# A weight row spread by transposes, a sum queued earlier and a shorter list of scans, in a hybrid decoder layer

## The chip, the cores and the metric

The kernel runs on one core of a Trainium2 chip. The metric is device time in microseconds of one execution, the median of several runs. TensorE (PE, with its weight loads as PEld), VectorE (DVE), ScalarE (ACT), GpSimd (POOL) and SyncE (SP, which issues most DMAs) each work through their own queue in order and wait for one another by semaphores.

## The reference

One decoder layer on 1024 tokens of width 1024, in float32:

```python
x = x + 0.5 * swiglu(rms_norm(x, ffn1_norm), ffn1_w_gate, ffn1_w_up, ffn1_w_down)   # d_ff 2816
h = rms_norm(x, mix_norm)
fq, fk, fv, f_logit, sq, sk, sv, g_fox, g_sb = split_columns(h @ w_in)
y_fox = forgetting_attention(rms_norm(fq), rms_norm(fk), fv, log_sigmoid(f_logit + bias))
y_sb = stick_breaking_attention(sq, sk, sv)
x = x + (sigmoid(g_fox) * (y_fox @ w_branch_fox) + sigmoid(g_sb) * (y_sb @ w_branch_sb)) @ w_out
x = x + 0.5 * swiglu(rms_norm(x, ffn2_norm), ffn2_w_gate, ffn2_w_up, ffn2_w_down)
x = x + sigmoid(rms_norm(x, ple_norm) @ w_ple_gate) * (p @ w_ple_proj)
```

Both attentions have 8 heads of 64 and are causal. In the stick-breaking one, a token's weight on an earlier one is `sigmoid(z)` times the product of `1 - sigmoid(z)` over the tokens between, which is a scan along each row of scores. `rms_norm` is `x * rsqrt(mean(x^2) + eps) * g`.

## The kernel before

Every float32 operand of a product is split into a high and a low part; a product is the sum of three (high by high, high by low, low by high). The feed-forward parts use products of sums of blocks, in an order written out by hand (`manual_schedule`): there the program's order is each engine's order.

**The entry** (`first_entry`) comes first. It loads x in eight tiles of 128 rows (`load_x`), and the weight row of the first norm into one partition of `gB`, by a DMA on ACT's queue (L1557). `busy(n)` (L253) issues n products of zeros of 128x512 in bf16, which nothing reads. `spread` (L239, L241) makes all 128 partitions of `gB` equal to the row: TensorE multiplies a column of ones with it, in two products of 512, and VectorE copies the two banks out. For each of the first four tiles `rows_stat` forms on ScalarE the mean of squares (L260, L262) and on GpSimd its power (L265), and `rows_mul` (L268, VectorE) the normed rows. `rows_high` turns a tile by eight transposes (L273) and copies the high part to `H` (L282, ScalarE); `rows_low` subtracts for the low part (L287, VectorE). `F.prep` splits weights (L600 ScalarE, L601 VectorE), and `F.plain` (L563) is the first product. In program order stand: `busy(8)`, `spread`, statistics and multiplies of four tiles, `busy(10)`, turns and splits, the first product, then the second half of x in the same way.

**Attention** is one loop over 16 heads (8 forgetting, then 8 stick-breaking), each in four steps `c` of 256 queries. Iteration `(h, c)` issues `scores` of its step, two rows of tiles of 128 queries, and between and behind them `apply` of the step two back; so the step with `c == 3` is applied while the next head's `c == 1` is scored. `fill()` puts products of other work (projections, L912 and L920) in between. Explicit order edges (`order`) hold TensorE to the program's order, and hold among themselves VectorE's scans, lower parts, sums and splits of y of the stick-breaking heads; the framework places the rest.

- `row` issues the score products (L1168, L1169), two sigmoids a bank (L1176, L1177), and leaves its scans (L1131) as parts of 256 columns in the list `pend`, sorted by step and then from the last columns to the first. A part ends with a multiply on GpSimd (L1200).
- `pop()` issues the first part of `pend`, two where more than five are pending; `pop(upto)` issues all up to a step and column.
- `apply` goes through pairs of 128 keys from the last to the first. `turn_and_scan` transposes the weights of a pair (L1228), copies the high part (L1230, ScalarE), pops scans, and subtracts for the low part (`low`, L1236, VectorE). `values` multiplies with v (L1254) into one bank, two pairs behind. At the end ScalarE copies half of the bank to y (L1280) and `add`, VectorE's sum of the other half (L1283), is left in the list `late`.
- `flush()` issues what is in `late`. After every second head, for odd `c`, `add` also calls `parts`, which splits y (L1296 ScalarE, L1297 VectorE) and issues two DMAs.

Of the kernel before, what the change touches and what calls it, by code (L numbers as in the profile page):

```python
# [10 lines left out]
F32 = mybir.dt.float32  # L11
# [7 lines left out]
P = 128  # L19
# [3 lines left out]
KD = D // P  # L23
# [13 lines left out]
def tile_hybrid_decoder_layer(  # L37
# [6 lines left out]
    nc = tc.nc  # L44
    cp = ctx.enter_context(tc.tile_pool(name="const", bufs=1))
# [10 lines left out]
    def slot(tag, shape, dt=F32):  # L56
        pad = -shape[-1] % 16
        t = sb.tile([*shape[:-1], shape[-1] + pad], dt, tag=tag, bufs=BUFS[tag], name=nm(tag))
        return t[:, :, :shape[-1]] if pad else t
# [20 lines left out]
    def pe(ins):  # L80
        order("pe", ins)
# [74 lines left out]
    nc.vector.memset(mhalf[:], -0.5)  # L156
    ones1 = cp.tile([P, 1], F32, name="ones1")
    nc.vector.memset(ones1[:], 1.0)
    gains = cp.tile([P, 3, KD], F32, name="gains")

    xd = dp.tile([KD, P, S], F32, name="x_mid")
    pd = dp.tile([KD, P, S], F32, name="p_proj")
# [67 lines left out]
    def rows_begin(X, gB):  # L230
        return {"rows": True, "x": X, "g": gB, "h": {}, "r": {}}

    def spread(gB):

        ones = slot("T", [1, P])
        nc.vector.memset(ones[:], 1.0)
        banks = [bank("sc") for _ in range(2)]
        for i, ps in enumerate(banks):
            pe(nc.tensor.matmul(ps[:], ones[:], gB[0:1, i * 512:i * 512 + 512], start=True, stop=True))  # L239
        for i, ps in enumerate(banks):  # L240
            nc.vector.tensor_copy(gB[:, i * 512:i * 512 + 512], ps[:])  # L241

# [887 lines left out]
    def scan(*args):  # L1130
        order("dve", nc.vector.tensor_tensor_scan(*args))  # L1131

    def pop(upto=None):

        n = 1 + (len(pend) > 5)
        while pend and (n if upto is None else pend[0][:2] <= upto):
            pend.pop(0)[2]()
            n -= 1
# [3 lines left out]
    def flush():  # L1142
        for call in [late.pop(0) for _ in range(len(late))]:
            call()

    def scores(step, fill):
        step["pr"] = []
        Q, KH, KL = step["st"]["st"]
        fox = step["fox"]

        def row(i):
            n = (i + 1) * P
            na, w = seg(n)
            d0 = n - P
            T = slot("T", [P, S])
            if fox:
                m = stat([P, 3], "m")
                l = stat([P, 1], "l")
                fb = step["fb"]["t"]
                nc.gpsimd.tensor_add(T[:, d0:n], fb[:, d0:n], mask_fox[:])  # L1160
                nm_ = 0
            else:
                G = slot(("GF", "RN")[i % 2], [P, S])
            for a in range(na) if fox else range(na - 1, -1, -1):
                c0, c1 = a * w, (a + 1) * w
                ps = bank("sc")
                q = Q[:, i * P:(i + 1) * P]
                pe(nc.tensor.matmul(ps[:, :w], q, KH[:, c0:c1], start=True, stop=False))  # L1168
                pe(nc.tensor.matmul(ps[:, :w], q, KL[:, c0:c1], start=False, stop=True))  # L1169
                if fox:  # L1170
                    for x0, x1, add in ((c0, min(c1, d0), fb), (max(c0, d0), c1, T)):
                        if x0 < x1:
                            nc.vector.tensor_tensor_reduce(T[:, x0:x1], add[:, x0:x1], ps[:, x0 - c0:x1 - c0], -1.0, m[:, nm_ - 1:nm_] if nm_ else 3e38, ALU.add, ALU.min, m[:, nm_:nm_ + 1])
                            nm_ += 1
                else:
                    nc.scalar.activation(G[:, c0:c1], ps[:, :w], AF.Sigmoid, scale=-(HD ** -0.5))  # L1176
                    nc.scalar.activation(T[:, c0:c1], ps[:, :w], AF.Sigmoid, scale=HD ** -0.5)  # L1177
            if fox:
                nc.scalar.activation(T[:, :n], T[:, :n], AF.Exp, bias=m[:, nm_ - 1:nm_], scale=-1.0, accum_out=l[:])
                nc.vector.reciprocal(l[:], l[:])  # L1180
                nc.gpsimd.tensor_mul(T[:, :n], T[:, :n], l[:].broadcast_to([P, n]))  # L1181
            else:
                nc.gpsimd.affine_select(T[:, d0:n], T[:, d0:n], [[-1, P]], ALU.is_ge, 0.0, base=-1, channel_multiplier=1)

                def part(kp, T=T, G=G, n=n, d0=d0):
                    c0 = kp * 256
                    c1 = min(c0 + 256, n)
                    z0 = max(c0, 1)
                    if c1 == n:
                        z1 = max(d0, 1)  # L1190
                        g = G[:, z1:n][:, ::-1]
                        scan(g, g, mask_sb[:, z1 - d0:P][:, ::-1], 1.0, ALU.mult, ALU.max)
                        if z0 < d0:
                            g = G[:, z0:d0][:, ::-1]
                            scan(g, g, g, G[:, d0:d0 + 1], ALU.mult, ALU.bypass)
                        c1 = n - 1
                    else:
                        g = G[:, z0:c1][:, ::-1]
                        scan(g, g, g, G[:, c1:c1 + 1], ALU.mult, ALU.bypass)
                    nc.gpsimd.tensor_mul(T[:, c0:c1], T[:, c0:c1], G[:, c0 + 1:c1 + 1])  # L1200
                pend.extend((step["id"], -kp, lambda kp=kp, part=part: part(kp)) for kp in range(step["c"], -1, -1))
                pend.sort(key=lambda e: e[:2])
            step["pr"].append(T)
            fill()
        for i in (2 * step["c"], 2 * step["c"] + 1):
            pop((step["id"] - 2, 0))
            pop()
            if fox or i % 2:
                flush()
            row(i)  # L1210
            yield

    def apply(step, fill):
        c = step["c"]
# [40 lines left out]

        def turn_and_scan(kpair):
            low = transposes(kpair)
            pop()
            pop((step["id"], 2 - kpair))
            low()  # L1260
            flush()
            fill()
# [285 lines left out]
    def first_entry(F):  # L1548

        X = [slot("X", [P, 4, D]) for _ in range(2)]  # L1550

        def load_x(t):
            nc.sync.dma_start(X[t // 4][:, t % 4, :], x_rows[0, t * P:(t + 1) * P, :])

        load_x(0)
        gB = slot("PT", [P, D])
        nc.scalar.dma_start(gB[0:1, :], ffn1_norm[0].unsqueeze(0))  # L1557
        nc.scalar.activation(stat([P, 1], "ss")[:], mhalf[:, 0:1], AF.Silu)
        N.append(rows_begin(X[0], gB))
        N.append(rows_begin(X[1], gB))  # L1560
        N[0]["B"] = [slot("H", [P, 2, 4, 512], F32R) for _ in range(2)]
        busy(0)
        busy(8)
        spread(N[0]["g"])
        for t in range(1, 4):
            load_x(t)
        F.load(0)
        for t in range(4, NT):
            load_x(t)
        F.load(1)  # L1570
        for i, gain in enumerate((mix_norm, ffn2_norm, ple_norm)):
            nc.sync.dma_start(gains[:, i, :], gain[0])
        for t in range(4):
            rows_stat(N[0], t, ("PT", "WL", "WL", "PT")[t], True)
            rows_mul(N[0], t)
        busy(10)
        rows_high(N[0], 0, ps1)
        rows_high(N[0], 1, ps1)
        rows_low(N[0], 0)
        F.prep(0, 1)  # L1580
        rows_high(N[0], 2, ps2)
        rows_low(N[0], 1)
        rows_high(N[0], 3, ps2)
        rows_low(N[0], 2)
        F.prep(0, 2)
        rows_stat(N[1], 0, "Y")
        rows_low(N[0], 3)
        rows_stat(N[1], 1, "Y")
        F.plain(0, 0, (0, 1), False)
        rows_mul(N[1], 0)  # L1590
        rows_stat(N[1], 2, "PT")
        rows_mul(N[1], 1)
        F.prep(0, 5)
        rows_stat(N[1], 3, "PT")
        F.prep(0, 4)
        rows_mul(N[1], 2)
        F.a(0)
        F.b(0, nc.vector)
        F.b(0)
        rows_mul(N[1], 3)  # L1600
        F.a(1)
        F.b(1, nc.vector)
        F.b(1)
        F.silu(0, 0)
        F.sums(1, nc.vector)
        F.load(2)
        for i in range(2):
            F.plain(1, 0, (i,))
            F.a(2 + i)
            F.b(2 + i, nc.vector)  # L1610
            F.b(2 + i)
            F.prep(1, 1 + i)
        F.prep(1, 5)
        ps = F.product(1, 1)
        F.t(0)
        F.evict(1, 1, ps)
        lower = F.prep(2, 1, True)
        F.t(1)
        F.l(0)
        lower()  # L1620
        ps = F.product(1, 2)
        F.t(2)
        F.l(1)
        F.t(3)
        F.l(2)
        F.evict(1, 2, ps)
        F.l(3)
        F.plain(0, 1)
        for fn in (F.u, lambda j: F.s(j, 6)):
            for j in range(2):  # L1630
                fn(j)
        F.prep(2, 2)
        F.plain(1, 1)
        for fn in (F.u, lambda j: F.s(j, 6)):
            for j in range(2, 4):
                fn(j)
        F.prep(1, 6)
# [218 lines left out]
```

## Time and profile before

| | us |
|---|---|
| median of 3 runs | 2238.27 (2237.66 to 2238.58) |
| the profiled execution | 2238.81 |
| its span | 2237.1 |
| busy TensorE / weight loads | 2214.9 / 1880.1 |
| busy VectorE | 1517.7 |
| busy ScalarE | 1006.2 |
| busy GpSimd | 822.8 |

In rows of the timeline the first number is the start in us from the span's start, the second the time from the first start to the last end, then engine, line, operation, tiles (out <- in), shapes and count; in brackets the idle time before it and what ended it. Rows of the stretches give, for each engine in turn (PE, PEld, DVE, ACT, POOL), busy time and instructions, then the granted clock, the DMA engines' share and GB/s. Rows of the waits give total us, times and the longest.

### The profile page before, as it was taken

The numbers are of one execution on the slowest core, as the hardware profiler recorded it, in microseconds if no ns is written. First come the engines' busy times: TensorE is split into PE (matmuls) and PEld (weight loads), VectorE is DVE, ScalarE is ACT, GpSimd is POOL, SyncE is SP. The second block draws the span as 40 slices with busy tenths as digits, with TensorE's granted clock in tenths as the row PEclk, the third lists the DMA queues.
The fourth block names the chain that finished last, engine by engine and source line by source line (L and its number), as shares of the span: only waits on it lengthen the run. The fifth ranks groups of instructions, "written<-read, shape, count | busy, mean of one in ns | idle before, by whom it ended". The sixth has DMA issues, their size and how long they took to land.

```text
span 2237.1 us, 30542 instructions
## 1 busy us (share of the span) xinstructions
PE 2214.9 (99%) x11212; PEld 1880.1 (84%) x11212; DVE 1517.7 (68%) x2367; ACT 1006.2 (45%) x1805; POOL 822.8 (37%) x788
## 2 busy tenths in 40 slices
PE   9999999999999999999999999999999999999999
PEld 7888888888888899999898888888888888888887
DVE  8855545598888324666677885789655555688888
ACT  6433333433455435555566663255333333333454
POOL 1344534210021336566567664520544444200021
PEclk9999999999999999999999999999999999999999
DMA  3332323394322334333323465741423232574336
GB/s 133 104 127 81 132 80 132 114 347 171 117 95 100 128 107 130 86 104 86 85 53 95 119 203 185 262 174 57 141 81 125 77 120 93 199 262 174 113 113 169
DMA packets 195607, 294.89 MB, mean 132 GB/s; under 512 B 28665, under 2 KB 108793, under 8 KB 195458
## 3 DMA queue, kind: packets, MB, share of 16 engines
q1 hardware_dynamic: 194448, 289.80, 39.3%
q0 software_dynamic: 1008, 3.15, 0.8%
q8 instruction: 88, 1.44, 0.3%
q14 instruction: 61, 0.50, 0.1%
q10 hardware_dynamic: 2, 0.00, 0.0%
HBM read 192.99 MB, written 83.13 MB: 123 GB/s over the span
## 4 chain that ended last, share of the span: by engine, by line
PE 93%; DVE 3%; ACT 2%; POOL 1%; issue 1%; DMA 0%; SPq 0%; ACTq 0%; DVEq 0%; POOLq 0%
PE ps L627 43%; PE ps L509 22%; PE ps L912 8%; PE ps L920 5%; PE ps L563 4%; PE ps L1523 3%; PE ps L1254 2%; PE ps L1228 2%; PE ps L1169 1%; PE ps L1168 1%; PE ps L1074 1%; DVE PT L1236 1%; DVE RN L1131 1%; DVE GF L1131 1%; POOL WL L139 0%
## 5 line engine op out<-in xcount | busy, mean ns | idle before, releaser
L509 PE MATMUL ps<-H,H 128*128 128x512 f32 x2184 | 497.3, 389 | 0.0
L509 PEld LDWEIGHTS ps<-H,H 128*128 128x128 f32 x2184 | 409.5, 188 | 84.8
L627 PE MATMUL ps<-H,WL 128*128 128x512 f32 x1164 | 275.0, 389 | 0.0
L627 PEld LDWEIGHTS ps<-H,WL 128*128 128x128 f32 x1164 | 218.5, 188 | 45.3
L185 POOL TENSOR_TENSOR PT<-PT,PT 128x512 f32<-128x512 f32 x27 | 34.9, 1294 | 403.9 <-ACT PT L182 403.0
L627 PE MATMUL ps<-H,Q 128*128 128x512 f32 x624 | 148.4, 389 | 0.0
L517 DVE SCALAR_TENSOR_TENSOR X<-ps,X 128x512 f32<-128x512 f32 x168 | 110.2, 685 | 47.2 <-PE ps L509 47.1
L627 PE MATMUL ps<-X,WL 128*128 128x512 f32 x576 | 138.3, 389 | 0.0
L627 PEld LDWEIGHTS ps<-H,Q 128*128 128x128 f32 x624 | 117.1, 188 | 24.3
L1236 DVE TENSOR_TENSOR PT<-ps,PT 128x512 fp32r<-128x512 f32 (+1 forms) x160 | 99.9, 628 | 44.2 <-ACT PT L1230 43.5
L627 PE MATMUL ps<-H,PT 128*128 128x512 f32 x540 | 128.9, 389 | 0.0
L627 PEld LDWEIGHTS ps<-X,WL 128*128 128x128 f32 x576 | 108.1, 188 | 22.4
L139 POOL TENSOR_TENSOR WL<-RAW,WH 128x512 fp32r<-128x512 f32 (+1 forms) x84 | 97.6, 1181 | 74.0 <-ACT WH L129 46.5
L412 POOL TENSOR_TENSOR PT<-GF,RN 128x512 f32<-128x512 f32 x20 | 33.5, 1674 | 236.8 <-DVE GF L820 236.8
L627 PEld LDWEIGHTS ps<-H,PT 128*128 128x128 f32 x540 | 101.2, 188 | 21.1
L912 PE MATMUL ps<-WH,H 128*128 128x256 f32 x768 | 116.1, 288 | 0.8 <-ACT RN L977 0.8
L920 PE MATMUL ps<-H,WH 128*128 128x512 f32 x384 | 115.0, 406 | 0.0
L1254 PE MATMUL ps<-PT,X 128*128 128x256 f32 (+1 forms) x640 | 102.4, 286 | 9.5 <-DVE PT L1236 8.6
L1230 ACT CAST PT<-ps 128x512 fp32r<-128x512 f32 (+1 forms) x160 | 87.2, 548 | 44.6 <-PE ps L1228 40.5
L1254 PEld LDWEIGHTS ps<-PT,X 128*128 128x128 f32 x640 | 90.3, 190 | 19.9 <-DVE PT L1236 13.4
L912 PEld LDWEIGHTS ps<-WH,H 128*128 128x128 f32 x768 | 101.5, 190 | 2.6 <-ACT RN L977 1.2
L1181 POOL TENSOR_TENSOR T<-T,l 128x128 f32<-128x128 f32 (+3 forms) x64 | 73.2, 1147 | 67.5 <-DVE l L1180 65.4
(453 smaller groups left out, 4795.9 us busy)
## 6 DMA issues: line engine op xcount, KB each, us to landing
hidden<-PT SPq DMA_DIRECT2D x40, 512.0 KB, 3.1
WH<-in_ffn_w_gate_dram SPq DMA_DIRECT2D x38, 512.0 KB, 5.5
Q<-hidden SPq DMA_DIRECT2D x24, 512.0 KB, 5.6
hidden<-RN SPq DMA_DIRECT2D x22, 512.0 KB, 2.6
KH<-in_ffn_w_up_dram SPq DMA_DIRECT2D x20, 512.0 KB, 6.2
KL<-in_ffn_w_up_dram SPq DMA_DIRECT2D x20, 512.0 KB, 6.9
T<-in_ffn_w_down_dram SPq DMA_DIRECT2D x20, 512.0 KB, 7.1
GF<-hidden SPq DMA_DIRECT2D x14, 512.0 KB, 7.0
```

What stands on the lines that cost most here:

```text
L139: ins = eng_lo.tensor_sub(lo[part], raw[part], f(hi[part]))
L509: pe(nc.tensor.matmul(groups[g][t][:], wt[:, b, k, t * P:(t + 1) * P], act[:, a, k, :], start=(fresh and n == 0), stop=(i in (6, 1, 4) and ...
L517: nc.vector.scalar_tensor_tensor(xs, groups[g][t][:], scale, xs, ALU.mult, ALU.add)
L563: pe(nc.tensor.matmul(ps[:], hl[:, a, k, :], right(rb, b, k), start=(i == 0), stop=(i == 23)))
L627: pe(nc.tensor.matmul(ps[:, cols], hl[:, a, k, :], right(B[m], b, k)[:, cols], start=(first and i == 0), stop=(final and i == 11), skip_gr ...
L912: pe(nc.tensor.matmul(ps[:, :n], hT[t // 4](a, k)[:, (t % 4) * P:(t % 4 + 1) * P], w[k // 4][b][:, k % 4, :n], start=(i == 0), stop=(i == ...
L920: pe(nc.tensor.matmul(ps[:], w[a][:, k, :], hT[half](b, k), start=(i == 0), stop=(i == 23)))
L1181: nc.gpsimd.tensor_mul(T[:, :n], T[:, :n], l[:].broadcast_to([P, n]))
L1230: high = nc.scalar.copy(pt[:, 0, :width], ps[:, :width])
L1236: ins = nc.vector.tensor_sub(pt[:, 1, :width], ps[:, :width], f(pt[:, 0, :width]))
L1254: pe(nc.tensor.matmul(o, lh, r, start=(kpair == c and i == 0), stop=(kpair == 0 and i == 3)))
L1523: pe(nc.tensor.matmul(ps[:], w[a][:, k, :], yT[g][b][:, k, half * 512:half * 512 + 512], start=(i == 0), stop=(i == 11)))
```

## The change

1. The weight of the first norm is laid out on the host as eight columns of 128 and loaded into `gains[:, 3, :]`, still from ACT's queue. `spread` makes the full rows by eight transposes of a column broadcast along the free axis, four to a bank. `busy(8)` before it becomes `busy(9)`, `busy(10)` behind the multiplies `busy(6)`. The memset of ones goes.
2. In `scores`, `flush()` is called ahead of both rows of a stick-breaking step; it was called ahead of the second alone. The sum of y left by the step before, and its split where there is one, then stand ahead of the first row.
3. `turn_and_scan` pops one part, not one or two, at the last two turns of a step with `c == 3`.

```diff
-    gains = cp.tile([P, 3, KD], F32, name="gains")
+    gains = cp.tile([P, 4, KD], F32, name="gains")
...
-    def spread(gB):
-
-        ones = slot("T", [1, P])
-        nc.vector.memset(ones[:], 1.0)
+    def spread(gB, col):
+
         banks = [bank("sc") for _ in range(2)]
-        for i, ps in enumerate(banks):
-            pe(nc.tensor.matmul(ps[:], ones[:], gB[0:1, i * 512:i * 512 + 512], start=True, stop=True))
+        for k in range(KD):
+            pe(nc.tensor.transpose(banks[k // 4][:, k % 4 * P:(k % 4 + 1) * P], col[:, k:k + 1].broadcast_to([P, P]), identf[:]))
         for i, ps in enumerate(banks):
             nc.vector.tensor_copy(gB[:, i * 512:i * 512 + 512], ps[:])
...
-    def pop(upto=None):
-
-        n = 1 + (len(pend) > 5)
+    def pop(upto=None, n=None):
+
+        n = n or 1 + (len(pend) > 5)
...
-            if fox or i % 2:
-                flush()
+            flush()
             row(i)
...
-            pop()
+            pop(n=1 if c == 3 and kpair < 2 else None)
             pop((step["id"], 2 - kpair))
...
-        nc.scalar.dma_start(gB[0:1, :], ffn1_norm[0].unsqueeze(0))
+        nc.scalar.dma_start(gains[:, 3, :], ffn1_norm[0])
...
-        busy(8)
-        spread(N[0]["g"])
+        busy(9)
+        spread(N[0]["g"], gains[:, 3, :])
...
-        busy(10)
+        busy(6)
...
-        elif name in ("mix_norm", "ffn2_norm", "ple_norm"):
+        elif name in ("ffn1_norm", "mix_norm", "ffn2_norm", "ple_norm"):
```

## The prediction

> **What bounds the kernel now.** I read the page first, then stretches, then the first 25 us engine by engine, then the waits and single steps of the stick-breaking part.
>
> ```profile
> span 2237.1 us, 30542 instructions
> ...
> PE 2214.9 (99%) x11212; PEld 1880.1 (84%) x11212; DVE 1517.7 (68%) x2367; ACT 1006.2 (45%) x1805; POOL 822.8 (37%) x788
> ...
> PE 93%; DVE 3%; ACT 2%; POOL 1%; issue 1%; DMA 0%; SPq 0%; ACTq 0%; DVEq 0%; POOLq 0%
> ```
> ```profile
> 50.00:635.00 585.00, 585.00 (x2585) 484.14 (x2584) 386.50 (x453) 218.36 (x337) 177.02 (x122) 1.00 0.39 136
> ...
> 1100.00:1345.00 245.00, 236.95 (x1448) 207.98 (x1447) 192.89 (x328) 154.20 (x339) 159.96 (x234) 1.00 0.42 115
> ```
>
> TensorE is the bound: 93% of the chain, and full from 50 to 635 us, where nothing of the diff runs. So an edit gains only where TensorE idles or does work that it need not: the first 18 us, and the stick-breaking part (1100 to 1345 us), where it is idle for 245 - 236.95 = 8 us. What is saved before 50 us is carried through the full stretch unchanged.
>
> **The entry (first edit).** The rows of TensorE:
>
> ```profile
> 1.32 3.59 PE L253 MATMUL ps<-T 128*128 128x512 bf16 x8 [1.32 <-DVE T L249]
> 4.84 3.78 PE L239 MATMUL ps<-PT,T 1*128 1x512 f32 x4
> 8.55 4.45 PE L253 MATMUL ps<-T 128*128 128x512 bf16 x10
> 12.79 1.67 PE L273 MATMUL ps<-identf,PT 128*128 128x128 f32 x8
> 14.30 1.91 PE L273 MATMUL ps<-identf,WL 128*128 128x128 f32 x16
> ...
> 18.09 5.78 PE L563 MATMUL ps<-H,WL 128*128 128x512 f32 x24 [1.01 <-ACT H L282]
> 23.71 1.91 PE L273 MATMUL ps<-identf,Y 128*128 128x128 f32 x16
> ```
>
> Filler products (L253) step by (12.79 - 8.55)/10 = 0.424 us; the same width at L563 steps by (23.71 - 18.09)/24 = 0.234. The first transposes take 0.21 each, the next sixteen 1.91/16 = 0.12. So the array runs at half pace until some point among the first transposes, though the column PEclk of the stretches reads 1.00: here the pace tells, not that column. What opens it matters below.
>
> ScalarE, then VectorE, GpSimd and the DMAs:
>
> ```profile
> 4.47 1.06 ACT L260 ACTIVATE PT<-X 128x1024 f32<-128x1024 f32 x1 [1.62 <-DMA X<-in_x_rows_dram]
> ...
> 7.72 1.06 ACT L260 ACTIVATE WL<-X 128x1024 f32<-128x1024 f32 x1 [0.55 <-DMA X<-in_x_rows_dram]
> ...
> 10.20 0.20 ACT L262 ACTIVATE ss<-ss 128x1 f32<-128x1 f32 x1
> 13.89 2.17 ACT L282 CAST H<-ps 128x512 fp32r<-128x512 f32 x4 [3.49 <-PE ps L273]
> 15.94 0.64 ACT L600 CAST WL<-WH 128x512 fp32r<-128x512 f32 x1
> 16.45 2.08 ACT L282 CAST H<-ps 128x512 fp32r<-128x512 f32 x4
> 18.36 0.68 ACT L600 CAST WL<-WH 128x512 fp32r<-128x512 f32 x1
> ```
> ```profile
> 8.66 0.69 DVE L241 COPY PT<-ps 128x512 f32<-128x512 f32 x1 [1.01 <-PE ps L239]
> 9.45 1.28 DVE L268 SCALAR_TENSOR_TENSOR PT<-X,rt,PT 128x1024 f32<-128x1024 f32 x1
> ...
> 13.04 1.28 DVE L268 SCALAR_TENSOR_TENSOR PT<-X,rt,PT 128x1024 f32<-128x1024 f32 x1
> ...
> 17.22 2.48 DVE L287 TENSOR_TENSOR H<-ps,H 128x512 fp32r<-128x512 f32 x4
> 19.61 0.68 DVE L601 TENSOR_TENSOR WL<-WH,WL 128x512 fp32r<-128x512 f32 x1
> ...
> 21.41 1.28 DVE L268 SCALAR_TENSOR_TENSOR Y<-X,rt,PT 128x1024 f32<-128x1024 f32 x1
> ```
> ```profile
> 10.48 0.66 POOL L265 TENSOR_TENSOR rt<-ss,mhalf 128x1 f32<-128x1 f32 x1 [0.74 <-ACT ss L262]
> ```
> ```profile
> 0.81 0.51 ACTq L1557 DMA_DIRECT2D PT<-in_ffn_norm_dram  x1
> ```
> ```profile
> gains<-in_ffn_norm_dram SPq DMA_DIRECT2D x1, 4.0 KB, 6.8
> ```
>
> Before: TensorE spends 3.7 us spreading the weight row (4.84 to 8.55), VectorE copies it out and multiplies until 14.32, the ten fillers hold TensorE until 12.79, and only then come the transposes; ScalarE waits 3.49 us for the first of them. The copies to H end in time for the first product at 18.09.
>
> After, step by step:
> - Nine fillers end at 1.32 + 9 x 0.424 = 5.14. The columns of the weight are issued on ACT's queue at 0.81, as the row is now. The same load for another norm lands within 6.8 us in the worst neighbourhood (behind megabytes on SP's queue); half a megabyte of x, issued at the same time on SP's queue, is read at 4.47, so I take the 4 KB to be there by 5.14, and it costs nothing. At 0.81 + 6.8 = 7.6 it would cost 2.5 us of the gain below, less what ScalarE's hole takes up.
> - Eight transposes at 0.21 end at 6.9; the second half of the row is complete about 0.2 later. The two copies (0.69) end at 7.8, the multiplies start at 7.9 instead of 9.45 and, at (13.04 - 9.45)/3 = 1.2 each, the last starts at 11.5 (its statistic is ready at 10.48 + 0.66 = 11.14) and ends at 12.8 instead of 14.32.
> - Six fillers end by 6.9 + 6 x 0.424 = 9.4, sooner if the clock opens; the first tile, ready at 9.2, is turned then. ScalarE is free at 10.40 (its statistics are set by the landing of x, which doesn't move), so its copies start at 10.40 instead of 13.89. The last tile (12.8) is turned before its copies are due at 10.40 + (16.45 - 13.89) + 1.0 = 13.95. The product, which waits for ScalarE, starts 3.49 earlier, at 14.6.
> - VectorE gains less. From 12.7 it has two H lows, a weight low, four H lows, then the second weight low. With no holes that is seven at 0.60, so the second weight low runs 16.9 to 17.6; the product wants it after twelve of its 24 steps, at 14.6 + 12 x 0.234 = 17.4. That is a wait of 0.3.
>
> The new bound is ScalarE with a little VectorE: 3.49 - 0.3 = **3.2 us saved**, between 3.5 and 0 (first rival).
>
> Behind 18 us the same order runs. ScalarE's rows name no wait for a DMA after 7.72, so I take the second half of x and the next weights to be there 3 us earlier too; if one is not, that much of the 3.2 is lost.
>
> **The sum of y (second edit).** In the stick-breaking part TensorE's waits are nearly all for one line, the lower part of transposed weights:
>
> ```profile
> PE ps L1254 <- DVE PT L1236: 7.2, 10, 1.3
> ```
> ```profile
> PEld ps L1254 <- DVE PT L1236: 9.9, 12, 1.5
> ```
>
> (The second counts the same waits on the weight loads.) VectorE's queue is in order. The edit moves `add` (L1283, 0.42 us) in every stick-breaking step from behind the first lower part to ahead of the step's first row, and in every fourth step the split of y (L1296, L1297) and its two DMA issues on SP with it. One step in which four pairs are turned, VectorE and ScalarE:
>
> ```profile
> 1177.84 0.39 DVE L1131 TENSOR_TENSOR_SCAN RN<-RN,mask_sb 128x128 f32<-128x128 f32 x1
> 1178.27 0.48 DVE L1131 TENSOR_TENSOR_SCAN RN<-RN 128x127 f32<-128x127 f32 x1
> 1180.26 0.42 DVE L106 TENSOR_TENSOR X<-ps,X 128x256 fp32r<-128x256 f32 x1 [1.51 <-ACT X L105]
> 1180.64 0.56 DVE L1236 TENSOR_TENSOR PT<-ps,PT 128x384 fp32r<-128x384 f32 x1
> 1181.22 0.42 DVE L1283 TENSOR_TENSOR Y<-ps,Y 64x256 f32<-64x256 f32 x1
> ...
> 1184.29 0.66 DVE L1236 TENSOR_TENSOR PT<-ps,PT 128x512 fp32r<-128x512 f32 x1
> ```
> ```profile
> 1178.67 0.37 ACT L1280 COPY Y<-ps 64x256 f32<-64x256 f32 x1 [3.86 <-PE ps L1254]
> ```
> ```profile
> 1184.11 1.52 PE L1254 MATMUL ps<-PT,X 128*128 128x256 f32 x8
> ```
>
> The sum cannot start before ScalarE's copy ends at 1179.04. After: it runs 1179.05 to 1179.47, the two scans that were done at 1178.75 wait behind it and end at 1180.4, a fill's 0.42 (L106) follows, and the first lower part starts at 1180.8, 0.15 late. From there the sum's 0.42 is gone, so the third (1184.29), for which TensorE waits within the row of eight, comes 0.27 earlier. So the sum moves into a hole, less what the scans lose there. Eight such steps: between 0 and 0.4 each; I take 0.15, 1.2 us, nearest to this row's 0.27 less the steps whose scans are longer. A step with a split:
>
> ```profile
> 1171.88 0.42 DVE L1283 TENSOR_TENSOR Y<-ps,Y 64x256 f32<-64x256 f32 x1
> 1173.02 0.99 DVE L1297 TENSOR_TENSOR Y<-Y,PT 128x512 fp32r<-128x512 f32 x1 [0.72 <-ACT PT L1296]
> ```
>
> Here 0.42 + 0.99 and the 0.72 of waiting go ahead of the first lower part, which is late by about 1.3 while later ones gain 0.5; the transposes that reuse its bank then wait. That nets to 0 within 0.5 in three such steps. The remaining steps turn one or two pairs and have slack: 0.2 in all. Sum **1.4 us saved**, between 0 and 2.6. In queue behind a waiting sum stand the scans, the lower parts and the fill's lows; who waits for them is L1254.
>
> **The part of scans (third edit).** `pop` takes two only when over five parts are pending. Following the list through all heads by the code, there are never more than five at the last two turns of a four-pair step. So `n=1` asks for what is done already: no instruction moves, 0 us.
>
> **Sum.** 3.2 + 1.4 = 4.6 us off the profiled execution's 2238.81 (span 2237.1 and 1.7 around it), 2234.2. The median of the runs, 2238.27, lies 0.54 under that execution: **2233.7**. About 0.2% (4.5 us, so 2233.8) is what a measurement here can tell from no change: the forecast lies on that edge.
>
> **Rivals.**
> 1. The clock opens late. Fillers of 3.4 us from 1.32 did not open it, ten fillers and some transposes (12.79 to about 14) did; so transposes seem to count, and the new unbroken stretch from 1.32 should open it by about 8. If they do not, six fillers are too few: the 32 transposes at 0.21 run from 9.4 to 16.1, the product starts at about 16.2 and its first eleven steps go at 0.424: 16.2 + 4.7 + 13 x 0.234 = 23.9 against 23.7 now. The entry gives 0; 2236.9. The Trainium skill, page "TensorE: Matmul & The Clock Gate", Part 4, says that transposes do not count as busy in the same way, which is this rival and would leave 1.4 of the sum. The trace does not agree as far as it goes: the pace changes amid transposes, between 12.79 and 14.30.
> 2. The sum stalls VectorE (slower). The point: where scans behind it push the first lower part past the point at which its products are due. With scans of 1 us and the split in the way every first lower part is 0.5 to 1.3 late; if that reaches TensorE at 0.3 in each of the 31 steps, that is 9.3 lost against 3.2: 2244.4. Against it: only four-pair and three-pair steps have waits now.
> 3. The sum gives nothing, what it frees is lost to the scans: 2235.1.
>
> **Chances.** Forecast mechanism 0.66 (2232.0 to 2235.0, its middle on the edge: 0.46 below, 0.20 within); rival 1 0.14; rival 3 0.08; rival 2 0.12. Faster 0.46, same 0.20 + 0.14 + 0.08 = 0.42, slower 0.12. The range runs from 2232.0 (3.5 and 2.6 with 0.1 over) to 2238.4, which takes in rival 1 with its phase of the clock and leaves out rival 2.
>
> **What would show it.** Right: L563's first product near 14.6, ScalarE's first H copy near 10.4 without the 3.49 wait, first transposes after the fillers at 0.12; L1283 ahead of the first L1236 in each step; L1131's order otherwise unchanged. Wrong: the eight column transposes waiting for a DMA, L563 stepping by 0.424, more waits of L1254 for L1236 than 9.9 us.

## Result and the profile after

The changed kernel takes **2232.07 us** (median of 9 runs, 2231.38 to 2232.84) against 2238.27 (9 runs beside them, 2236.14 to 2239.49): ratio 0.9974, 95% interval [0.9964, 0.9984]. Its profiled execution took 2232.07 with a span of 2230.4, 6.7 us under the span of before. The forecast was 2233.7, in a range from 2232.0 to 2238.4, with "faster" the likeliest. So it came out faster, as forecast, but 1.6 us below the forecast and 0.07 inside the lower end of the range. The parts did not come out as forecast: the entry was overrated and the sum of y underrated.

The head of the page of after, then TensorE's rows of the entry (start, length, line, tiles, idle time ahead and its releaser; lines stand two or three lower than before):

```profile
span 2230.4 us, 30521 instructions
...
PE 2210.9 (99%) x11213; PEld 1879.4 (84%) x11213; DVE 1516.2 (68%) x2366; ACT 1005.5 (45%) x1805; POOL 818.1 (37%) x788
```
```profile
1.32 4.02 PE L251 MATMUL ps<-T 128*128 128x512 bf16 x9 [1.32 <-DVE T L247]
5.13 1.75 PE L237 MATMUL ps<-identf,gains 128*128 128x128 f32 x8
6.72 1.46 PE L251 MATMUL ps<-T 128*128 128x512 bf16 x6
9.05 1.09 PE L271 MATMUL ps<-identf,PT 128*128 128x128 f32 x8 [0.88 <-DVE PT L266]
...
14.05 3.03 PE L561 MATMUL ps<-H,WL 128*128 128x512 f32 x12 [0.25 <-ACT H L280]
17.43 3.03 PE L561 MATMUL ps<-H,WL 128*128 128x512 f32 x12 [0.35 <-DVE WL L599]
```

The first nine fillers step at 0.42, the last six at 1.46/6 = 0.24: the clock opens in between, at 6.57, where the eight transposes of columns stand. (The trace's record of the clock begins with this opening. Ahead of it the clock column of the stretches reads 1.00 for want of a record.) The transposes of the first tile then take 1.09/8, not 0.21 each, and the first product starts at 14.05 (before: 18.09). Next, ScalarE and VectorE:

```profile
7.13 1.06 ACT L258 ACTIVATE WL<-X 128x1024 f32<-128x1024 f32 x1
...
9.74 2.27 ACT L280 CAST H<-ps 128x512 fp32r<-128x512 f32 x4
```
```profile
6.23 1.38 DVE L239 COPY PT<-ps 128x512 f32<-128x512 f32 x2 [4.97 <-PE ps L237]
7.71 1.28 DVE L266 SCALAR_TENSOR_TENSOR PT<-X,rt,PT 128x1024 f32<-128x1024 f32 x1
...
25.28 1.28 DVE L266 SCALAR_TENSOR_TENSOR PT<-X,rt,PT 128x1024 f32<-128x1024 f32 x1 [0.64 <-POOL rt L263]
```

ScalarE has no hole ahead of its H copies any more; they start at 9.74. The last row is new: VectorE waits 0.64 for a statistic of the second half. The stick-breaking stretch, and its waits (total, times, longest):

```profile
1100.00:1345.00 245.00, 239.41 (x1462) 210.35 (x1460) 193.76 (x327) 156.32 (x345) 155.85 (x239) 1.00 0.42 115
```
```profile
PEld ps L1251 <- DVE PT L1233: 7.6, 12, 1.5
PE ps L1251 <- DVE PT L1233: 4.6, 8, 1.3
```

TensorE is busy 239.41 of 245 us where it was busy 236.95, and its waits for lower parts fell from 7.2 to 4.6.

Where the 6.7 us between the two profiled executions come from: the start of each product of TensorE in after less that of the same product in before.

| at (us) | shift | since the row above |
|---|---|---|
| 30 | -3.42 | entry |
| 50 to 1100 | -2.74 | +0.68 at about 31 us |
| 1350 | -5.30 | -2.56, stick-breaking steps |
| 1380 to the end | -6.73 | -1.43, at one place near 1373 us |

The last step was not foreseen. Before, then after, ScalarE's rows at that place (PT casts are the high parts of transposed weights):

```profile
1373.00 1.06 ACT L1666 ACTIVATE KL<-KL 128x1024 f32<-128x1024 f32 x1 [3.01 <-DMA KL<-gates]
1373.96 1.05 ACT L1230 CAST PT<-ps 128x512 fp32r<-128x512 f32 x2
```
```profile
1364.77 0.59 ACT L1227 CAST PT<-ps 128x512 fp32r<-128x512 f32 x1
1368.70 1.06 ACT L1663 ACTIVATE KL<-KL 128x1024 f32<-128x1024 f32 x1 [3.34 <-DMA KL<-gates]
1369.66 1.05 ACT L1227 CAST PT<-ps 128x512 fp32r<-128x512 f32 x2
```

The gate's sigmoid waits for a DMA in ScalarE's queue. Before, two casts stood behind it and TensorE waited for their result; the row of TensorE in before reads

```profile
1375.40 0.63 PE L1228 MATMUL ps<-identf,T 128*128 128x128 f32 x4 [1.72 <-DVE PT L1236]
```

With the second edit the kernel's own ordering of ScalarE's work puts one cast ahead of the sigmoid, and TensorE's wait there is 0.4. No edit names this line.

### The profile page after: what moved, and what is told of

It reads as the page before. It is cut to its first block, busy times and chain, and to the rows that moved or that the text cites. A ratio compares the mean times of both kernels' runs of the same rounds, so it can differ in the third digit from the quotient of the medians.

```text
span 2230.4 us, 30521 instructions
## 1 busy us (share of the span) xinstructions
PE 2210.9 (99%) x11213; PEld 1879.4 (84%) x11213; DVE 1516.2 (68%) x2366; ACT 1005.5 (45%) x1805; POOL 818.1 (37%) x788
## 3 DMA queue, kind: packets, MB, share of 16 engines
q8 instruction: 88, 1.44, 0.3%
## 5 line engine op out<-in xcount | busy, mean ns | idle before, releaser
L625 PEld LDWEIGHTS ps<-X,WL 128*128 128x128 f32 x576 | 108.1, 188 | 22.4
L1251 PEld LDWEIGHTS ps<-PT,X 128*128 128x128 f32 x640 | 90.4, 190 | 18.0 <-DVE PT L1233 11.5
```

Source lines behind the costliest of these rows:

```text
L625: pe(nc.tensor.matmul(ps[:, cols], hl[:, a, k, :], right(B[m], b, k)[:, cols], start=(first and i == 0), stop=(final and i == 11), skip_gr ...
L1251: pe(nc.tensor.matmul(o, lh, r, start=(kpair == c and i == 0), stop=(kpair == 0 and i == 3)))
```

## Experiments

Times are medians; the ratio is to runs of the kernel before on the same chip.

**1. The entry alone.** `gains` of four columns, `spread(gB, col)`, fillers 9 and 6; nothing else.

> The kernel before with the first edit alone (columns turned instead of the row spread, 9 and 6 fillers). Theory: the entry's saving stands by itself, and GpSimd's scaling of gqk, which stands ahead of the last statistics after the edit, takes some of it back: TensorE is 3.4 us earlier at 25 us and 2.7 us earlier from 35 us to the end, so 2.7 us under the kernel before, and nothing changes at 1373 us. Rival: the entry also moves something at 1373 us (4.1 under), or what is gained before 50 us is used up later (0 to 1 under).

Measured: 2236.72 (11 runs) against 2237.88, ratio 0.9995 [0.9986, 1.0004]. In the trace TensorE is 3.30 earlier at 30 us and 2.62 earlier from 50 to 1440 us, as the theory says, and nothing moves at 1373 us. But 0.95 goes again between 1440 and 1510 us. ScalarE waited at 1430 us for a tile of `w_out` (the DMA view; last, us from issue to landing):

```profile
Y<-in_w_out_dram SPq DMA_DIRECT2D x1, 512.0 KB, 6.0
```

In before and after it landed in 5.6. Six of the fourteen profiled executions lose 0.7 to 0.95 there; in these six the tile landed 6.0 to 6.4 after its issue, in the others 4.9 to 5.9. By the medians the entry is worth 1.2, with 0 inside the interval.

**2. The sum alone.**

```
-            if fox or i % 2:
-                flush()
+            flush()
```

> The kernel before with the second edit alone (the sum of y ahead of every row). Theory: 2.6 us in the stick-breaking steps up to 1345 us and 1.4 us at about 1373 us, where ScalarE's gate sigmoid falls one weight cast later: 4.0 us under the kernel before. Rival A, the prediction's size: 1.4 us, all in the steps, and the 1.4 us at 1373 us comes from the shift of the entry. Rival B: the steps give nothing without the entry's shift (0).

Measured: 2232.42 (8 runs), ratio 0.9977 [0.9966, 0.9987], 5.5 us. The stretch of the profile:

```profile
1100.00:1345.00 245.00, 239.51 (x1463) 210.38 (x1462) 194.11 (x331) 156.30 (x345) 155.15 (x236) 1.00 0.42 116
```

That is the whole gain of the stretch without the entry: TensorE is 2.7 earlier at 1350 us than at 1100, and 1.44 more at 1373 us. The theory holds, and rivals A and B fall. The medians give 1.4 more than the 4.1 of the trace. The profiled execution (2234.70) is the longest of its eight, and its clock opened late, at 12.60; five of the eight took 2231.62 to 2232.46, no longer than the changed kernel. Experiment 3 shows what a late clock costs, and experiment 6 what else may make up the difference.

**3. The scans alone.**

```
-            pop()
+            pop(n=1 if c == 3 and kpair < 2 else None)
```

> The kernel before with the third edit alone (one part of scans ahead of the last lower parts of a four-pair step). Theory: no instruction moves, 0 within 0.5 us, and the order of the scans' line is the same. Rival: the edit holds scans back there and gives some of what the stick-breaking part gained (1 us or more).

Measured: 2238.13 (11 runs), ratio 1.0001 [0.9992, 1.0010]. The order of every engine's instructions is that of before, so this is a second profile of the same program, and it does not look like the first:

```profile
1.32 3.60 PE L253 MATMUL ps<-T 128*128 128x512 bf16 x8 [1.32 <-DVE T L249]
4.85 2.19 PE L239 MATMUL ps<-PT,T 1*128 1x512 f32 x4
6.97 2.33 PE L253 MATMUL ps<-T 128*128 128x512 bf16 x10
9.20 1.10 PE L273 MATMUL ps<-identf,PT 128*128 128x128 f32 x8
...
15.28 3.04 PE L563 MATMUL ps<-H,WL 128*128 128x512 f32 x12 [0.24 <-ACT H L282]
```

The row spread takes 2.19 instead of 3.78, the ten fillers 2.33 instead of 4.45, and the first product starts at 15.28 instead of 18.09. The trace's record of the granted clock has it open at 5.30 us here and at 14.08 in the profile that the prediction was made from. From 50 us on TensorE is 1.67 earlier, with no instruction moved. So 1.7 of the entry's 2.6 is not always there to be won.

What is left has another source. The product is 1.23 later here than in after, and so is the third tile of x, for which ScalarE waits until 8.36 (7.13 in after):

```profile
8.36 1.06 ACT L260 ACTIVATE WL<-X 128x1024 f32<-128x1024 f32 x1 [1.01 <-DMA X<-in_x_rows_dram]
```

In the eleven profiles whose clock opened by 7.41, with the edit or without, the product starts 6.7 to 7.2 after ScalarE takes up this tile. ScalarE does so at 7.08 to 7.41 in the nine profiles that load the weight as columns, and at 7.44 to 8.78 in the five that load it as a row. Why x is later beside the row is not shown.

**4. The gate's sigmoid alone**, in the kernel before: fixed behind the weight casts.

```
-            nc.scalar.activation(gs[m][:], gs[m][:], AF.Sigmoid)
+            order("act", nc.scalar.activation(gs[m][:], gs[m][:], AF.Sigmoid))
```

> The kernel before, with the one place of ScalarE's gate sigmoid alone changed: it is put behind the weight casts that it stood ahead of. Theory: TensorE's wait of 1.9 us at about 1373 us goes to 0.4 or less, 1.4 to 1.9 us under the kernel before, and nothing else changes. Rival: the wait there is set by the gates' transfer or by VectorE's queue, so the sigmoid's place changes nothing (0), and the 1.4 us of the changed kernel has another cause.

Measured: 2236.49 (11 runs), ratio 0.9991 [0.9982, 0.9999]. TensorE is level with before up to 1370 us (-0.01) and 1.93 earlier from 1380 us on. The rival falls: the sigmoid's place alone makes the wait.

**5. Only transposes ahead of the product**, in the changed kernel.

```
-        for _ in range(n):
-            pe(nc.tensor.matmul(ps[:], zero[0][:, 0:P], zero[0][:], start=True, stop=True))
+        for i in range(2 * n):
+            pe(nc.tensor.transpose(ps[:, i % 4 * P:(i % 4 + 1) * P], identf[:], identf[:]))
```

> The changed kernel with each filler product replaced by two transposes of the identity, as long (0.21 each at half pace), so that only transposes and no bf16 product run ahead of the first product of H. Theory: transposes count for the clock, so it opens between 4.7 and 8.2 us as with fillers, the pace of the transposes goes from 0.21 to 0.11 there, and the first product is at 14.0 within 0.4; total as the changed kernel (2232 within 1). Rival (transposes do not count): 0.21 each up to the product, its first steps at 0.42, the product starts 1 to 2 later and is 2 longer, total 2235 to 2237.

```profile
1.54 4.10 PE L251 MATMUL ps<-identf 128*128 128x128 f32 x18 [1.54 <-POOL identf masks.py:199]
5.43 1.91 PE L237 MATMUL ps<-identf,gains 128*128 128x128 f32 x8
7.14 1.61 PE L251 MATMUL ps<-identf 128*128 128x128 f32 x12
...
14.52 3.03 PE L561 MATMUL ps<-H,WL 128*128 128x512 f32 x12 [0.25 <-ACT H L280]
```

The clock opened at 7.41 with nothing but transposes behind it: their pace goes from 4.10/18 = 0.23 to 1.61/12 = 0.13, and the product starts at 14.52, 0.12 later than the theory's limit. Transposes count. The Trainium skill, page "TensorE: Matmul & The Clock Gate", Part 4, says that they do not; the measurement decides. The total was still 2236.92 (10 runs; before 2236.83, ratio 0.9999 [0.9989, 1.0008]). The rival had put it there too, but its reason, a late clock, did not come about: the loss lies behind the product. GpSimd's order came out different here:

```profile
20.74 0.22 POOL L1641 TENSOR_SCALAR gqk<-gqk 64x1 f32<-64x1 f32 x1 [3.91 <-DMA gqk<-in_q_norm_dram]
20.94 0.56 POOL L263 TENSOR_TENSOR rt<-ss,mhalf 128x1 f32<-128x1 f32 x1
```
```profile
21.00:24.40 3.40, 1.09 (x8) 0.85 (x8) 2.10 (x2) 0.84 (x2) 3.15 (x4) 1.00 0.00 0
24.50:27.90 3.40, 2.98 (x11) 2.77 (x12) 3.40 (x6) 2.82 (x7) 2.94 (x4) 0.50 0.36 71
```

The scaling of `gqk` stood ahead of the power of the second half's first statistic and waited for its load. TensorE was busy 1.09 of 3.4 us, and for the next 3.4 us its granted clock (third column from the end) was 0.50. TensorE, 3.6 ahead at 20 us, was 1.8 behind before at 30 us. The Trainium skill, the same page, Part 1, says that the clock is set by free-running windows of 3.4 us; this stretch agrees (24.47 to 27.89, 3.413 us before rounding).

**6. The counts alone**, in the kernel before: `busy(9)` and `busy(6)`, the row still spread by its one-row products.

> The kernel before with the counts of fillers alone changed (9 and 6 for 8 and 10); the row is still spread by the one-row products. It divides the first edit in two. Theory A, the fillers held the array: four of them at 0.42 less, so the first transposes start at 11.4 in place of 12.8, ScalarE's first copy at 12.3 and the product at 16.7, 1.4 under the kernel before, if the clock opens by then (fillers from 8.95 are in its favour); the columns give the other 1.3. Theory B, VectorE's multiplies are the bound (the last ends at 14.3 or 0.4 later, since one more filler goes ahead): 0.5 under to 0.4 over.

Measured: 2238.02 (10 runs) against 2236.83, ratio 1.0000 [0.9990, 1.0009]. The clock opened at 5.33 in this execution, the product started at 14.43, and TensorE was 2.57 ahead from 50 us, nearly as much as with the columns. Neither theory had that. The 0.9 beyond experiment 3 (1.67) is not the work of the fillers: ScalarE takes up the third tile of x at 7.44, 0.92 earlier than there. Then, near 1373 us:

```profile
1370.00:1374.00 4.00, 2.17 (x15) 1.79 (x14) 1.86 (x3) 2.38 (x4) 0.00 (x0) 1.00 0.25 74
1374.00:1377.50 3.50, 3.50 (x14) 3.12 (x13) 0.71 (x2) 0.23 (x1) 0.00 (x0) 0.51 0.73 194
```
```profile
1372.98 0.63 PE L1228 MATMUL ps<-identf,T 128*128 128x128 f32 x4 [1.83 <-DVE PT L1236]
...
1374.17 0.63 PE L1523 MATMUL ps<-X,WH 128*128 128x512 f32 x1
1374.60 0.63 PE L1523 MATMUL ps<-H,WH 128*128 128x512 f32 x1
```

The wait behind the sigmoid left TensorE idle for 1.83 in one window, and the clock was 0.51 in the next: products step at 0.43. That costs 1.7 (the shift goes from -2.53 to -0.86). The profile of before had nearly the same wait, 1.72, and kept its clock. In windows of 3.41 us, counted on from the opening of each, TensorE was busy for 1.59 us in the window with the wait here and for 1.69 us in that of before. So the wait costs 1.9 in some executions (experiment 4) and, by an estimate from these two numbers (1.9 and 1.7), up to 3.6 in others. The second edit cuts the wait to 0.4, and no profile with that edit has a drop here. One execution shows the drop; how often it happens was not counted.

**7. The columns alone**, in the kernel before, with the counts 8 and 10.

> The kernel before with the columns turned but the old counts of fillers, 8 and 10. Theory: the clock opens at 5 to 8.5 us amid transposes and fillers, so the ten fillers cost at most 0.23 each beyond that point and end by 10 us, when ScalarE is not yet free for its copies (9.74 with the whole change); the product starts within 0.3 of 14.05 and the entry is 2.4 to 2.75 under the kernel before from 50 us on, so the counts are worth 0.3 or less. Rival: the ten fillers hold the transposes by 0.42 each, 1.4 to 1.7 of the saving goes.

Measured: 2236.55 (10 runs) against 2236.83, ratio 0.9997 [0.9987, 1.0006]. The ten fillers end at 8.9, the product starts at 13.95, and TensorE is 2.70 ahead from 50 us. The theory holds: in this profile the counts are worth nothing once the columns are turned; the medians cannot tell, with 0 inside the interval. (This execution is 1.1 further ahead at 1373 us, where its gates landed earlier, and lost 0.7 at the tile of `w_out`; the medians keep neither.)

**8. The scaling of gqk behind the last power**, in the changed kernel (an order for GpSimd on these two lines).

> The changed kernel with one placement on GpSimd reversed: gqk's scaling (2.39) goes behind the power of the last statistics in place of ahead of it. Theory: VectorE's wait of 0.64 for rt at 25 us and TensorE's of 0.41 at 31.7 us go, TensorE stays 3.4 earlier than before (not 2.75) from 35 us on, 0.65 under the changed kernel. Rival: something else bounds the second half's rows (x's landing or ScalarE), 0 to 0.2.

Measured: 2231.76 (8 runs), ratio 0.9973 [0.9963, 0.9983]; 0.15 ahead of after from 50 us.

```profile
22.39 2.73 POOL L263 TENSOR_TENSOR rt<-ss,mhalf 128x1 f32<-128x1 f32 x1
25.10 0.25 POOL L1641 TENSOR_SCALAR gqk<-gqk 64x1 f32<-64x1 f32 x1
```

The rival is right. The power took 2.73 where it took 0.56 behind the scaling, so whichever goes first at 22.4 is long, and VectorE still waits 0.46. In experiment 3, in the old order, the second half loses 0.5 at the same place.

What makes GpSimd slow there shows beside VectorE's rows:

```profile
23.94 0.75 DVE L661 TENSOR_TENSOR T<-Q,T 128x256 fp32r<-128x256 f32 x2
25.15 1.29 DVE L266 SCALAR_TENSOR_TENSOR PT<-X,rt,PT 128x1024 f32<-128x1024 f32 x1 [0.46 <-POOL rt L263]
```

The long power ends at 25.12, 0.43 after VectorE's run of instructions that read two tiles (L266, L599, L661) ends at 24.69. This holds throughout: from 2 to 60 us the fourteen profiles have 182 such powers and scalings on GpSimd. 113 of them are short (powers 0.54 to 0.59, scalings 0.22 to 0.36). The other 69 take 0.66 to 2.73, and each ends 0.08 to 0.09 or 0.41 to 0.43 after the end of such an instruction on VectorE. While VectorE runs L285, which reads one tile and a bank, they are short. So GpSimd seems to wait for VectorE there; no run moved VectorE's work to test it.

**9 to 12. The changed kernel again, and three steps beyond it.** Each builds on the one before; 10 adds experiment 4's line to 8, 11 takes `eng=nc.gpsimd` for the second weight's lower part, and 12 is

```
+            first = c == 3 and kpair < 2 and not step["fox"]
+            if first:
+                low()
             pop(n=1 if c == 3 and kpair < 2 else None)
             pop((step["id"], 2 - kpair))
-            low()
+            if not first:
+                low()
```

> The changed kernel once more, as the measure for the three kernels beside it and as a second look at its entry. Theory: the clock opens between 4.7 and 8.2 us whatever its phase, the first product starts within 0.5 of 14.05, 2232.1 within 0.5. Rival: its entry too has a second state (clock at 10 us or later), 1 to 2 us over, in some runs.

> The changed kernel with gqk's scaling behind the last power on GpSimd and the gate sigmoid behind the last weight cast on ScalarE. Theory: the wait of 0.39 at 1371 us goes too, 0.3 to 0.4 under the kernel with gqk alone, 0.6 to 0.8 under the changed kernel. Rival: the product behind waits for the gates' sum instead, or the time that gqk frees is taken by the power (2.73 in the run with gqk alone): 0.1 to 0.3 under the changed kernel.

> As the last, and the second weight's lower part of the entry runs on GpSimd in place of VectorE, so the product's wait of 0.35 at 17.4 us goes. Theory: another 0.3, about 1 under the changed kernel. Rival: GpSimd takes 1.4 where VectorE takes 0.68 and holds its statistics' powers behind it, so the second half's rows are late by as much: 0.3 under to 0.5 over.

> As the last, and in the last two turns of every four-pair stick-breaking step the lower part of the transposed weights goes ahead of the part of scans in place of behind it. Theory: the largest waits left in the stick-breaking part (1.49, 0.88, 0.75, 0.66) are for a lower part behind scans of up to 1.9, each becomes 0.6 to 1.1 shorter, 2 to 3 us in all. Rival: VectorE then idles until ScalarE's cast is done, the scans end later and the next step's first turns wait for them: 0, or 1 to 3 slower.

| kernel | median (runs) | ratio to before, 95% |
|---|---|---|
| before, beside them | 2238.36 (15) | |
| 9, changed kernel | 2231.94 (7) | 0.9972 [0.9961, 0.9983] |
| 10 | 2231.35 (7) | 0.9968 [0.9957, 0.9979] |
| 11 | 2230.84 (6) | 0.9966 [0.9954, 0.9979] |
| 12 | 2228.04 (4) | 0.9954 [0.9939, 0.9969] |

Kernel 9's profiled execution opened its clock at 4.0 us, earlier than the theory's 4.7 to 8.2, and started its product at 13.77. No late start was seen, and its runs (2231.10 to 2232.25) leave no room for the rival's 1 to 2 us. Kernel 10 is 0.48 faster at 1373 us, and in the entry of its profiled execution 0.28 behind after; its 0.6 by the medians is the theory's lower end, but its runs (2231.23 to 2232.61) overlap those of kernel 9. Kernel 11's product runs through without the 0.35, another 0.5 by the medians; GpSimd takes 1.30 for the lower part, and TensorE is still 0.43 ahead of after at 30 us. Kernel 12 gains 2.8 more. First VectorE's rows of after at the largest wait left, then those of kernel 12:

```profile
1243.27 0.56 DVE L1129 TENSOR_TENSOR_SCAN RN<-RN,mask_sb 128x128 f32<-128x128 f32 x1
1243.87 1.33 DVE L1129 TENSOR_TENSOR_SCAN RN<-RN 128x128 f32<-128x128 f32 x1
1245.12 0.66 DVE L1233 TENSOR_TENSOR PT<-ps,PT 128x512 fp32r<-128x512 f32 x1
```
```profile
1241.62 0.66 DVE L1233 TENSOR_TENSOR PT<-ps,PT 128x512 fp32r<-128x512 f32 x1
1242.20 1.22 DVE L1129 TENSOR_TENSOR_SCAN RN<-RN,mask_sb 128x128 f32<-128x128 f32 x1
1243.46 0.68 DVE L1129 TENSOR_TENSOR_SCAN RN<-RN 128x128 f32<-128x128 f32 x1
1244.06 0.66 DVE L1233 TENSOR_TENSOR PT<-ps,PT 128x512 fp32r<-128x512 f32 x1
```
```profile
1100.00:1345.00 245.00, 241.93 (x1477) 212.97 (x1476) 196.89 (x331) 159.12 (x353) 156.99 (x242) 1.00 0.42 115
```
```profile
PEld ps L1251 <- DVE PT L1233: 4.0, 7, 1.0
PE ps L1251 <- DVE PT L1233: 1.9, 4, 0.7
```

In after the lower part at 1245.12 stands behind two scans, and TensorE waits 1.3 for it. In kernel 12 it runs ahead of the scans, the scans stay in time, and the stretch is busy for 2.5 us more. The theory's 2 to 3 holds. This is the best version found: 10.3 under before, 3.9 under the changed kernel.

## Why the prediction was right, point by point

- **The total** lies inside the range by luck. Its two terms were both wrong, in opposite directions: 3.2 for the entry and 1.4 for the sum, against 2.7 and 4.0 between the two profiled executions, and 0.3 to 1.2 (experiments 1 and 7) and 5.5 (experiment 2) by the medians. The errors cancel only in part: 6.2 was saved in place of 4.6, of which 1.4 in the profile came from a place that no term covered.
- **The entry's steps** came as worked out. The columns' load cost nothing, the eight transposes ended at 6.88 (6.9 was forecast), the multiplies started at 7.71 (7.9), the last began at 11.31 (11.5), and the wait for the second weight low was 0.35 (0.3). One did not: "ScalarE is free at 10.40 (... the landing of x, which doesn't move)". ScalarE took up the third tile of x 0.6 earlier, the copies started at 9.74, and so the product at 14.05 and not 14.6. By experiment 3 this point scatters, and it was later in every profile that loads the row.
- **"Behind 18 us the same order runs"** failed by 0.68, but not through a DMA, as the text feared: GpSimd is the limit at 22 to 25 us, with the scaling ahead of the last power or behind it, most likely because it waits for VectorE (experiment 8).
- **What the entry is worth** failed most. The step at fault is the base: one profile of before was taken for the kernel. Its clock opened at 14.08; in the same order of instructions (experiment 3) it opened at 5.30, and there the entry has 2.62 - 1.67 = 0.95 to give, all of it by way of the third tile of x. Other executions with the old entry opened at 13.82 (experiment 4) and 12.60 (experiment 2). With the columns turned and bf16 fillers ahead of them, eight profiled executions open at 4.0 to 6.8. The forecast of 3.2 had a lower end of 0 for another reason, a late clock after the change.
- **The sum's 1.4** was mis-sized. In the four-pair step that was worked through, after has the first lower part at 1178.14 and the third at 1181.20; against before less its shift of 2.8 that is 0.3 later and 0.3 earlier (0.15 and 0.27 were forecast). The term that was wrong is the step with a split ("That nets to 0 within 0.5 in three such steps"). In before, TensorE's two waits behind a split in a four-pair step are

```profile
1239.79 0.62 PE L1254 MATMUL ps<-PT,X 128*128 128x256 f32 x3 [0.74 <-DVE PT L1236]
```
```profile
1302.73 0.62 PE L1254 MATMUL ps<-PT,X 128*128 128x256 f32 x3 [0.74 <-DVE PT L1236]
```

  and both fall by 0.63 in after (from 0.90 to 0.27 by the starts of the products): the second lower part no longer has the split and ScalarE's copy ahead of it. In the third, at 1175 us, the predicted wait for the bank came, as long as the one it replaced. So splits gave 1.3 and not 0, and all other steps the remaining 1.3, about what was forecast for them.
- **The gate's sigmoid** was missing. The working counted what moves on VectorE and SP and took ScalarE's order for granted; the edit moved the sigmoid by one cast, which is 1.4 in the profile and more where the clock drops behind the wait (experiment 6).
- **The scans** at 0 were right (experiment 3).
- **Rival 1** (the clock opens late) fell in experiment 5, **rival 2** (the sum stalls VectorE) and **rival 3** (it gives nothing) in experiment 2. The sign of rival 2 was near at hand in the first lower part, which is 0.3 late, but TensorE does not wait for that one.

## What to carry to other kernels

A single profile is one draw. Where single runs scatter by as much as the effect (before 2235.5 to 2241.3 in 83 runs, the changed kernel 2231.1 to 2232.8 in 16), ask which waits and which clock the profile happened to catch before pricing an edit from it. An in-order queue that holds a wait for a DMA (here a sigmoid) sets the price of all that is put behind it, so check that place on every engine when a change shifts the order anywhere. And work that somebody waits for goes ahead of work that has slack: by the medians, lower parts ahead of scans gave more than the entry did.

## What the runs showed of the hardware

- Transposes open TensorE's clock: with no other product ahead of it, it opened at 7.41 us (experiment 5).
- What counts is not one long stretch but how full a window of 3.41 us is, counted from the opening. In the fourteen profiles the clock opened at the end of the first window that fillers and transposes filled for 79% or more (79% of fillers alone in experiment 9, at 4.0; 58% of fillers and 42% of transposes in after, at 6.57). It stayed shut behind all windows with 74% of them or less. In six of these TensorE was busy throughout, with one-row products in the rest, among them 38% in before at 10.67 (14.08 less one window), 27% in experiment 2 at 5.77, 46% in experiment 4 at 10.41. That one-row products count less is the reading that fits all of them; it was not tested by itself.
- A wait of 1.83 us in TensorE can cost 1.7 more at half clock in the next 3.4 us (experiment 6). A wait of 1.72 in another execution cost nothing beyond itself.
- A 128x1 power on GpSimd took 0.56 in one place of the queue and 2.73 in another. All long ones end 0.08 to 0.43 after an instruction of VectorE that reads two tiles (experiment 8).
